# RMSNorm with every row written twice: the first load issued by itself, gamma in small pieces, and the first tile's rows dealt in another order

## The chip, the cores and the metric

The kernel runs on one core of a Trainium2 chip. The core has a vector engine (DVE), a scalar engine (ACT), a general engine (POOL), a matrix engine (PE, unused here) and a sync engine (SP) that only issues transfers and waits. All transfers, whichever engine issues them, are carried out by the same 16 DMA engines. The metric is the time of one execution on the device in microseconds (us). Before the change three runs took 239.03, 238.68 and 238.97 us: a median of 238.97.

## The reference

```python
x_rep = np.repeat(x, 2, axis=1)                      # x: (8, 512, 2048) float32
rms = np.sqrt((x_rep ** 2).mean(axis=-1, keepdims=True) + 1e-6)
return (x_rep / rms * gamma[None, None, :]).astype(np.float32)
```

There are 4096 rows of 2048 numbers. Each row is divided by its root mean square and multiplied by gamma, and the result is written twice, to two neighbouring rows of an output of 8192 rows. A row has 8 KB, so 33.6 MB are read and 67.1 MB are written.

## The kernel before

The rows are cut into four tiles of 1024 rows (`n` = 0 to 3). Each of the 128 partitions takes eight neighbouring rows of a tile: 64 KB that lie in one piece in memory. So a load is one transfer of 128 runs of 64 KB, 8.4 MB. The sixteen rows that a partition writes for a tile go out in two halves (`h` = 0, 1) of eight rows each, so a store is again 128 runs of 64 KB.

One buffer `y` of 24 rows a partition holds everything (line 46), in three places of eight rows, `first` (rows 0 to 7), `second` (8 to 15) and `third` (16 to 23). The order of instructions is written out by hand. `four(n, ...)` handles two tiles, and it is called twice, for tiles 0 and 1 and for tiles 2 and 3. In it:

- `load(n, first + K)` brings tile n into rows 4 to 11 (line 50), `constants()` runs the first time only, and `load(n + 1, third)` brings the next tile into rows 16 to 23. Both loads are issued by SP, one after the other, and share one queue with the stores.
- `squares` sums the squares of each row on ACT (line 63) and takes the root (line 67). `scale` takes the reciprocal on DVE (line 73) and multiplies row, reciprocal and gamma (line 75) into every second row of the output. `repeat` copies these rows to their neighbours, on ACT or DVE (line 82).
- `store` sends eight rows from SP (line 53). There are eight stores, two for each tile.

So the SP queue carries, in this order: load 0, load 1, four stores, load 2, load 3, four stores. SP issues in order: what waits there holds up all that stands behind it. Each of these twelve transfers is shared out to the 16 DMA engines, eight runs of 64 KB to each, which makes 96 runs an engine in all. A run appears in the profile as one packet.

`constants()` (lines 116 to 126) issues gamma from ACT in two pieces of 4 KB into partition 0 of `gamma_b` (line 118), which POOL then broadcasts to all partitions (line 122). DVE sets `eps_t` (line 123). ACT takes one square root of it into a tile of its own, `root`, whose value nobody uses (line 126): it makes ACT load its function table early.

Of the kernel before, what the change touches and what calls it, by code (L numbers as in the profile page):

```python
# [1 line left out]

# [4 lines left out]


@with_exitstack
def kernel(  # L10
    ctx: ExitStack,
    tc: tile.TileContext,
    x: bass.AP,
    gamma: bass.AP,
    out: bass.AP,
):
    nc = tc.nc
    P = nc.NUM_PARTITIONS
    f32 = mybir.dt.float32
    Act = mybir.ActivationFunctionType  # L20
    Alu = mybir.AluOpType

    B, S, D = x.shape
    Bo, So, Do = out.shape
    R = So // S
    assert R == 2 and D == Do and B == Bo and So == S * R
    eps = 1e-6
    inv_d = 1.0 / float(D)


    K = 4
    N = B * S
    ntiles = N // (P * K)
    assert N % (P * K) == 0 and ntiles == 8
    H = 2
    x_t = x.rearrange("b s d -> (b s) d").rearrange("(n p k) d -> n p k d", p=P, k=H * K)
    out_t = out.rearrange("b s d -> (b s) d").rearrange("(n p h j) d -> n h p (j d)", p=P, h=H, j=K * R)

    singles = ctx.enter_context(tc.tile_pool(name="singles", bufs=1))
    rows = ctx.enter_context(tc.tile_pool(name="rows", bufs=1))  # L40
    junk = ctx.enter_context(tc.tile_pool(name="junk", bufs=1, space=bass.MemoryType.PSUM))
    small = ctx.enter_context(tc.tile_pool(name="small", bufs=4))

    y = rows.tile([P, 3 * K * R, D], f32, name="y")
    first, second, third = 0, K * R, 2 * K * R

    def load(n, at):
        nc.sync.dma_start(out=y[:, at : at + H * K, :], in_=x_t[n])  # L50

    def store(n, h, to):
        nc.sync.dma_start(
            out=out_t[n, h], in_=y[:, to : to + K * R, :].rearrange("p j d -> p (j d)")
        )

    def squares(at, rows):

        n = len(rows)
        ss = small.tile([P, n], f32, name=f"ss{n}")  # L60
        for c, k in enumerate(rows):
            sq = junk.tile([P, D], f32, name="sq")
            nc.scalar.activation(  # L63
                out=sq[:], in_=y[:, at + k, :], func=Act.Square, accum_out=ss[:, c : c + 1]
            )
        rms = small.tile([P, n], f32, name=f"rms{n}")
        nc.scalar.activation(out=rms[:], in_=ss[:], func=Act.Sqrt, scale=inv_d, bias=eps_t[:])  # L67
        return rms

    def scale(at, to, rows, rms):  # L70
        n = len(rows)
        rstd = small.tile([P, n], f32, name=f"rstd{n}")
        nc.vector.reciprocal(out=rstd[:], in_=rms[:])  # L73
        for c, k in enumerate(rows):
            nc.vector.scalar_tensor_tensor(  # L75
                out=y[:, to + R * k, :], in0=y[:, at + k, :], scalar=rstd[:, c : c + 1],
                in1=gamma_b[:], op0=Alu.mult, op1=Alu.mult,
            )

    def repeat(to, k0, k1, copy):  # L80
        y_r = y[:, to + R * k0 : to + R * k1, :].rearrange("p (k r) d -> p k r d", r=R)
        copy(out=y_r[:, :, 1, :], in_=y_r[:, :, 0, :])  # L82

    ctx.enter_context(tc.manual_schedule())

    half = K // 2
    up, down = list(range(K)), list(range(K - 1, -1, -1))

    def four(n, constants):


        load(n, first + K)
        constants()
        load(n + 1, third)
        for rows in (up[:half], up[half:]):
            scale(first + K, first, rows, squares(first + K, rows))
        repeat(first, 0, half, nc.scalar.copy)
        repeat(first, half, K, nc.vector.tensor_copy)
        store(n, 0, first)
        scale(second, second, down, squares(second, down))  # L100
        repeat(second, half, K, nc.scalar.copy)
        repeat(second, 0, half, nc.vector.tensor_copy)
        store(n, 1, second)
        roots = [squares(third + h * K, up) for h in range(H)]
        scale(third, first, up, roots[0])
        repeat(first, 0, half, nc.scalar.copy)
        repeat(first, half, K, nc.scalar.copy)
        store(n + 1, 0, first)
        scale(third + K, third, up, roots[1])
        repeat(third, 0, K, nc.scalar.copy)  # L110
        store(n + 1, 1, third)

    gamma_b = singles.tile([P, D], f32, name="gamma_b")
    eps_t = singles.tile([P, 1], f32, name="eps_t")

    def constants():
        for c0 in (0, D // 2):
            nc.scalar.dma_start(
                out=gamma_b[0:1, c0 : c0 + D // 2],
                in_=gamma[c0 : c0 + D // 2].partition_broadcast(1),  # L120
            )
        nc.gpsimd.partition_broadcast(out_ap=gamma_b[:], in_ap=gamma_b[0:1, :])  # L122
        nc.vector.memset(eps_t, eps)  # L123

        root = singles.tile([P, 1], f32, name="root")
        nc.scalar.activation(out=root[:], in_=eps_t[:], func=Act.Sqrt)  # L126

    four(0, constants)
    four(2, lambda: None)


# [1 line left out]
_INS = ['x', 'gamma']  # L133
_OUTS = [((8, 1024, 2048), 'float32')]


# [23 lines left out]
```

## Time and profile before

| What | Value |
|---|---|
| median of three runs | 238.97 us (238.68 to 239.03) |
| span of the profiled execution | 236.7 us |
| time of the profiled execution itself | only the span is recorded; the median lies 2.2 us above it |
| DVE busy | 84.4 us, 36% of the span |
| ACT busy | 110.2 us, 47% |
| POOL busy | 2.5 us, 1% |
| SP's queue (q1): share of 16 DMA engines | 98.5%, 1728 packets, 100.66 MB |
| ACT's queue (q10), the two pieces of gamma | 4 packets, 0.01 MB |
| mean rate over the span | 425 GB/s |

A transfer leaves two kinds of packets: the data, 64 KB each here, and one of 4 bytes for each DMA engine when its share is done. In the lines on DMA the window asked for is cut into 40 equal slices, and a packet is put down, with all its bytes and all its time, to the slice in which it starts. In short slices, therefore, the row "GB/s" tells when packets begin: a packet of 65536 bytes in a slice of 0.04 us shows as 1638. For the same reason the shares of a short window can be over 100%. Share times length of the window times 16, over the number of packets, is the mean time of a packet.

### The profile page before, as it was taken

How to read it: one execution, taken by the hardware profiler on the slowest of the kernel's cores; microseconds unless marked ns; L12 is line 12 of the kernel's file. 1: busy time of each engine (PE TensorE's matmuls, PEld its weight loads, DVE VectorE, ACT ScalarE, POOL GpSimd, SP SyncE). 2: the span in 40 equal slices, each digit the busy share in tenths (PEclk: the TensorE clock that was granted, in tenths of full speed). 3: DMA queues.
4: the chain of work that ended last, by engine and by line, in shares of the span. 5: the costliest groups of instructions: out<-in, count | busy, mean ns of one | idle time of the engine just before them, and what ended most of it. 6: DMA issues, size and time to landing. Idle time of an engine off the chain costs nothing.

```text
span 236.7 us, 218 instructions
## 1 busy us (share of the span) xinstructions
DVE 84.4 (36%) x47; ACT 110.2 (47%) x86; POOL 2.5 (1%) x5
## 2 busy tenths in 40 slices
DVE  0000495594699400000000008929909992000000
ACT  2001989479998460000000058991999947300000
POOL 0210000000000000000000000000000000000000
DMA  9898989999898989899898989899898989899894
GB/s 355 355 532 354 532 354 487 399 443 443 365 520 354 532 354 509 377 465 421 354 532 354 532 354 520 367 399 487 354 532 354 520 365 509 376 465 421 365 520 177
DMA packets 1733, 100.68 MB, mean 425 GB/s; under 512 B 194, under 2 KB 194, under 8 KB 196
## 3 DMA queue, kind: packets, MB, share of 16 engines
q1 hardware_dynamic: 1728, 100.66, 98.5%
q10 hardware_dynamic: 4, 0.01, 0.0%
q14 instruction: 1, 0.01, 0.0%
HBM read 33.56 MB, written 67.11 MB: 425 GB/s over the span
## 4 chain that ended last, share of the span: by engine, by line
DMA 45%; ACT 26%; DVE 13%; issue 1%; DVEq 0%; SPq 0%
DMA y<-in_x_dram 26%; DMA out_dram<-y 20%; ACT sq L63 15%; DVE y L75 13%; ACT y L82 11%; ACT rms L67 1%; DVE rstd L73 0%; DVEq L75 0%; SPq L50 0%
## 5 line engine op out<-in xcount | busy, mean ns | idle before, releaser
L63 ACT ACTIVATE sq<-y 128x2048 f32<-128x2048 f32 x32 | 60.1, 1878 | 72.0 <-DMA y<-in_x_dram 71.3
L75 DVE SCALAR_TENSOR_TENSOR y<-y,rstd,gamma_b 128x2048 f32<-128x2048 f32 x32 | 73.8, 2349 | 2.1 <-DMA out_dram<-y 1.5
L82 ACT COPY y<-y 128x4096 f32<-128x4096 f32 (+1 forms) x10 | 42.6, 4283 | 19.5 <-DVE y L75 19.5
L73 DVE RECIPROCAL rstd<-rms 128x4 f32<-128x4 f32 (+1 forms) x10 | 1.7, 170 | 109.0 <-ACT rms L67 109.0
L82 DVE COPY y<-y 128x4096 f32<-128x4096 f32 x4 | 9.2, 2293 | 0.1
L63 ACT ACTIVATION_READ_ACCUMULATOR sq<-y 128x1 f32 x32 | 6.0, 186 | 0.0
L67 ACT ACTIVATE rms<-ss,eps_t 128x4 f32<-128x4 f32 (+1 forms) x10 | 3.0, 297 | 0.3
L122 POOL PARTITION_BROADCAST gamma_b<-gamma_b x1 | 2.3, 2294 | 10.2 <-DMA gamma_b<-in_gamma_dram 10.2
L126 ACT ACT_TABLE_LOAD x1 | 1.3, 1283 | 1.5 <-PEq L144 1.5
L123 DVE MEMSET eps_t<- 128x1 f32 x1 | 0.1, 59 | 0.8 <-PEq L144 0.8
L126 ACT ACTIVATE root<-eps_t 128x1 f32<-128x1 f32 x1 | 0.2, 203 | 0.0
L144 POOL MEMSET const-bfloat16-1.0<- 128x1 bf16 x1 | 0.1, 103 | 0.0
L144 POOL MEMSET const-float32-0.0<- 128x1 f32 x1 | 0.1, 100 | 0.2 <-issue 0.2
L144 POOL MEMSET const-uint8-127<- 128x1 uint8 x1 | 0.1, 102 | 0.0
L144 POOL MEMSET const-float32-1.0<- 128x1 f32 x1 | 0.1, 99 | 0.0
## 6 DMA issues: line engine op xcount, KB each, us to landing
out_dram<-y SPq DMA_DIRECT2D x8, 24.8
y<-in_x_dram SPq DMA_DIRECT2D x4, 39.2
gamma_b<-in_gamma_dram ACTq DMA_DIRECT2D x2, 4.0 KB
```

What stands on the lines that cost most here:

```text
L63: nc.scalar.activation(out=sq[:], in_=y[:, at + k, :], func=Act.Square, accum_out=ss[:, c : c + 1])
L67: nc.scalar.activation(out=rms[:], in_=ss[:], func=Act.Sqrt, scale=inv_d, bias=eps_t[:])
L73: nc.vector.reciprocal(out=rstd[:], in_=rms[:])
L75: nc.vector.scalar_tensor_tensor(out=y[:, to + R * k, :], in0=y[:, at + k, :], scalar=rstd[:, c : c + 1], in1=gamma_b[:], op0=Alu.mult, op ...
L82: copy(out=y_r[:, :, 1, :], in_=y_r[:, :, 0, :])
L122: nc.gpsimd.partition_broadcast(out_ap=gamma_b[:], in_ap=gamma_b[0:1, :])
L123: nc.vector.memset(eps_t, eps)
L126: nc.scalar.activation(out=root[:], in_=eps_t[:], func=Act.Sqrt)
L144: nc = _bacc.Bacc("TRN2", target_bir_lowering=False, num_devices=1)
```

## The change

Four things are edited.

- The first tile (`woven = (0,)`) is read and written through `x_w` and `out_w`. Partition p = 8w + q, with w from 0 to 15 and q from 0 to 7, now takes run 16q + w of the tile, where it took run p. The partitions with equal q in the 16 groups of eight thus take 16 neighbouring runs of 64 KB; before, eight neighbouring runs lay within one group, and the groups were 512 KB apart. On the memory's side the pattern has the dimensions 16 x 8 x 16384 elements; on the side of `y` it stays 128 partitions by 16384. The two stores of tile 0 write through the same order, with runs of 64 KB that are 128 KB apart from group to group (1 MB before). Tiles 1 to 3 keep their order.
- The unused square root writes `y[:, third, 0:1]`, the place that load 1 fills. Load 1 therefore waits on SP until ACT has done that square root.
- On ACT the table load and the square root now stand ahead of the DMA issues for gamma.
- Gamma comes as 16 pieces of 125 numbers (500 bytes) in one transfer and three transfers of 16 numbers (64 bytes) each. They land in rows 0 to 2 of partition 0 of `y`, with 1 KB between the starts of the 16 pieces, and two broadcasts on POOL, of 2000 and of 48 columns, bring them into `gamma_b`.

```diff
+    woven = (0,)
+    W = 16
+    x_w = x.rearrange("b s d -> (b s) d").rearrange("(n q w k) d -> n w q (k d)", w=W, q=P // W, k=H * K)
+    out_w = out.rearrange("b s d -> (b s) d").rearrange("(n q w h j) d -> n h w q (j d)", w=W, q=P // W, h=H, j=K * R)
+
     def load(n, at):
-        nc.sync.dma_start(out=y[:, at : at + H * K, :], in_=x_t[n])
+        to = y[:, at : at + H * K, :].rearrange("p k d -> p (k d)")
+        nc.sync.dma_start(out=to, in_=x_w[n] if n in woven else x_t[n].rearrange("p k d -> p (k d)"))
 
     def store(n, h, to):
         nc.sync.dma_start(
-            out=out_t[n, h], in_=y[:, to : to + K * R, :].rearrange("p j d -> p (j d)")
+            out=(out_w if n in woven else out_t)[n, h], in_=y[:, to : to + K * R, :].rearrange("p j d -> p (j d)")
         )
...
     gamma_b = singles.tile([P, D], f32, name="gamma_b")
+    G, E = 16, 3
+    C = D // G - E
+    gamma_s = y[0:1, 0:2, :].rearrange("p k (c d) -> p (k c) d", c=G // 2)
+    gamma_t = y[0:1, 2, :]
     eps_t = singles.tile([P, 1], f32, name="eps_t")
 
     def constants():
-        for c0 in (0, D // 2):
-            nc.scalar.dma_start(
-                out=gamma_b[0:1, c0 : c0 + D // 2],
-                in_=gamma[c0 : c0 + D // 2].partition_broadcast(1),
-            )
-        nc.gpsimd.partition_broadcast(out_ap=gamma_b[:], in_ap=gamma_b[0:1, :])
         nc.vector.memset(eps_t, eps)
 
-        root = singles.tile([P, 1], f32, name="root")
-        nc.scalar.activation(out=root[:], in_=eps_t[:], func=Act.Sqrt)
+        root = y[:, third, 0:1]
+        nc.scalar.activation(out=root, in_=eps_t[:], func=Act.Sqrt)
+        nc.scalar.dma_start(
+            out=gamma_s[0:1, :, :C],
+            in_=gamma[: G * C].rearrange("(p c d) -> p c d", p=1, c=G),
+        )
+        for c in range(E):
+            at = G * C + c * G
+            nc.scalar.dma_start(
+                out=gamma_t[0:1, c * G : (c + 1) * G],
+                in_=gamma[at : at + G].partition_broadcast(1),
+            )
+        nc.gpsimd.partition_broadcast(
+            out_ap=gamma_b[:, : G * C].rearrange("p (c d) -> p c d", c=G),
+            in_ap=gamma_s[0:1, :, :C],
+        )
+        nc.gpsimd.partition_broadcast(out_ap=gamma_b[:, G * C :], in_ap=gamma_t[0:1, : E * G])
```

More of the change, by code (lines that the diff above doesn't have):

```diff
@@ L113 @@
     gamma_b = singles.tile([P, D], f32, name="gamma_b")
+    G, E = 16, 3
+    C = D // G - E
+    gamma_s = y[0:1, 0:2, :].rearrange("p k (c d) -> p (k c) d", c=G // 2)
+    gamma_t = y[0:1, 2, :]
     eps_t = singles.tile([P, 1], f32, name="eps_t")
     def constants():
-        for c0 in (0, D // 2):
+        nc.vector.memset(eps_t, eps)
+        root = y[:, third, 0:1]
[6 more added lines that the diff above has]
+            at = G * C + c * G
             nc.scalar.dma_start(
-                out=gamma_b[0:1, c0 : c0 + D // 2],
-                in_=gamma[c0 : c0 + D // 2].partition_broadcast(1),
-            )
-        nc.gpsimd.partition_broadcast(out_ap=gamma_b[:], in_ap=gamma_b[0:1, :])
-        nc.vector.memset(eps_t, eps)
-        root = singles.tile([P, 1], f32, name="root")
-        nc.scalar.activation(out=root[:], in_=eps_t[:], func=Act.Sqrt)
+                out=gamma_t[0:1, c * G : (c + 1) * G],
+                in_=gamma[at : at + G].partition_broadcast(1),
+            )
+        nc.gpsimd.partition_broadcast(
[3 more added lines that the diff above has]
+        nc.gpsimd.partition_broadcast(out_ap=gamma_b[:, G * C :], in_ap=gamma_t[0:1, : E * G])
     four(0, constants)
```

## The prediction

> **What bounds the kernel now.** I read the page first: span, busy shares, queues.
>
> ```profile
> span 236.7 us, 218 instructions
> ...
> DMA  9898989999898989899898989899898989899894
> ...
> q1 hardware_dynamic: 1728, 100.66, 98.5%
> q10 hardware_dynamic: 4, 0.01, 0.0%
> ```
>
> SP's queue keeps the 16 DMA engines busy 98.5% of the span; no other engine passes 47%. So the time is the queue's length: when it starts, how long its packets take, when it ends. Next, the DMA view of a stretch in the middle, 24 to 60 us, which holds the end of load 1 and the start of the stores:
>
> ```profile
> DMA packets 255, 15.66 MB, mean 435 GB/s; under 512 B 16, under 2 KB 16, under 8 KB 16
> ...
> q1 hardware_dynamic: 255, 15.66, 100.4%
> ```
>
> There is no hole: 435 GB/s over 16 engines is 2.41 us for 64 KB. Then the start, in two windows that hold just the first and the second packet of each engine (1.6 to 3.2 us in slices of 0.04 us, where one packet shows as 1638; and 4.4 to 5.6 us in slices of 0.03 us, one packet 2185):
>
> ```profile
> GB/s 102 0 0 6554 3277 1638 1638 6554 1638 0 0 0 0 0 1638 0 0 0 0 0 0 0 0 1638 0 0 0 0 0 0 0 0 1638 0 0 0 0 0 0 0
> ...
> q1 hardware_dynamic: 16, 1.05, 187.7%
> q10 hardware_dynamic: 2, 0.00, 0.6%
> ```
>
> ```profile
> GB/s 0 0 0 0 0 0 0 0 0 4369 0 2185 0 2185 2185 2185 2185 2185 2185 2185 0 0 4369 2185 0 2185 0 0 2185 0 2185 0 0 0 0 0 0 0 0 0
> ...
> q1 hardware_dynamic: 16, 1.05, 201.6%
> ```
>
> Thirteen engines start between 1.72 and 1.96 us (mean of the slices 1.83); three are late, at 2.18, 2.54 and 2.90. The mean first packet takes 1.877 x 1.6 = 3.00 us, the mean second 2.016 x 1.2 = 2.42 us. The second packets start at 4.67 to 5.33, mean 4.96. Had all started like the thirteen and taken 2.42 us, the second would start at 4.16 to 4.36, mean 4.25. So the start loses 0.53 us on the first engine, 0.71 on the mean and 0.96 on the last, and nothing gives that back in a queue without holes.
>
> Are there other such places? At the turn from stores to load 2 (115.6 to 119.6 us, two packets an engine) and at the end (231.8 to 236.7, slices of 0.12 us, one packet 535):
>
> ```profile
> GB/s 0 655 1311 1966 2621 0 1311 1311 1311 0 0 0 0 0 0 0 0 0 0 0 0 0 0 0 0 0 0 0 1311 655 1966 1966 3932 655 0 0 0 0 0 0
> ...
> q1 hardware_dynamic: 48, 2.10, 128.3%
> ```
>
> ```profile
> GB/s 0 0 535 3210 2675 1070 535 0 0 0 535 0 0 0 0 0 0 0 0 0 0 0 0 0 0 0 0 0 0 0 0 0 0 0 0 0 0 0 0 0
> ```
>
> There 32 data packets take 1.283 x 4 x 16 / 32 = 2.57 us in the mean, 0.15 too much, twice: 0.3 us an engine. The change does not touch this place. At the end one engine starts its last packet at 233.0 to 233.2, some 0.4 us after the rest, and ends at 235.5; 1.2 us later the span is over. The floor is 1.74 + 96 x 2.42 = 234.1, so the slowest engine has lost 1.4 us altogether, of which the start is the largest part. Last, the timeline of the first microseconds and the chain, for the cover of what is moved:
>
> ```profile
> 0.72 0.76 ACTq L118 DMA_DIRECT2D gamma_b<-in_gamma_dram  x2
> 0.72 0.86 SPq L50 DMA_DIRECT2D y<-in_x_dram  x2
> ...
> 1.51 1.28 ACT L126 ACT_TABLE_LOAD   x1 [1.51 <-PEq L144]
> 2.80 0.20 ACT L126 ACTIVATE root<-eps_t 128x1 f32<-128x1 f32 x1
> 10.59 2.29 POOL L122 PARTITION_BROADCAST gamma_b<-gamma_b  x1 [10.16 <-DMA gamma_b<-in_gamma_dram]
> 22.61 1.88 ACT L63 ACTIVATE sq<-y 128x2048 f32<-128x2048 f32 x1 [19.61 <-DMA y<-in_x_dram]
> ...
> 27.27 4.62 DVE L75 SCALAR_TENSOR_TENSOR y<-y,rstd,gamma_b 128x2048 f32<-128x2048 f32 x2
> ...
> 39.15 0.35 SPq L53 DMA_DIRECT2D out_dram<-y  x1
> ```
>
> **The change part by part.**
>
> *Load 1 waits for the square root.* SP issued it about 0.43 us after load 0 (0.86 us for two). Now it waits for table load and root: 1.28 + 0.20 us, so done at 2.2 us if the table load moves up to 0.72, at 3.0 if it stays. Issue (0.43) and the way to the first packet (0.72 to 1.74: 1.0 us) bring it to the engines by 4.5 at the latest. They need it after eight packets, at 1.74 + 8 x 2.42 = 21.1. Cover 16.6 us; cost nothing. Behind it on SP stands the first store, at 39.15. ACT's four DMA issues for gamma (0.38 each, 1.5 us in all) end before 5 us; ACT sits idle until 22.61.
>
> *Gamma's bytes.* The two pieces before went to one engine: two packets, 4 KB and its completion, took 0.006 x 1.6 x 16 = 0.15 us, so 0.31 us for both pieces. Now every engine presumably carries 500 bytes and a completion, and one engine three times 64 bytes on top. Price: from 500/4096 of 0.15, which is 0.02, to 0.15 us an engine, and up to 0.45 more on the one with the three. I take 0.04 on each, nearest to the bytes. It is a loss: the engine that carried 0.31 before was one of sixteen, and the end shows no spread that only it would explain.
>
> *Gamma's arrival.* In the 6 to 12 us window the second piece's 4 KB start at 7.5 to 7.7, and POOL starts at 10.59: between data and completion lay one 64 KB packet. Four transfers are eight such turns. The first can fall at 6.6 (after two 64 KB packets), the eighth at 6.6 + 7 x 2.42 = 23.5; 0.5 us later POOL does the 48 columns, in 2.29 us at most (that is 2048 columns), so gamma is complete by 26.3 and probably by 24.5. The first broadcast, 2000 columns, runs at about 9.5 to 12. DVE needs gamma at 27.27 minus whatever load 0 gains, 26.3 to 26.7. It fits, though the cover shrinks from 14 us to two at best and none at worst; a miss of 1 us would still be taken by the next cover: store 0 is issued at 39.15 and needs 1.0 us to its first packet, and the earliest engine is free at 4.67 + 15 x 2.42 = 40.97, so 0.8 us to spare. After a full cure load 0 lands 0.96 earlier on the last engine and the earliest engine is free 0.53 earlier, which leaves 1.2 us.
>
> *The dealt order, load 0.* Nothing in the number or size of packets changes: eight of 64 KB an engine. What can change is the first round (3.00 against 2.42 us) and the three late starts. Bounds: a gain of 0.96 us (last engine, all cured) and none. That later packets of the same load, 0.65 us apart from first to last engine, run at 2.42 us says that the loss comes from sixteen engines reading in step, and that points to where they read; the late starts could be the other two transfers issued in the same microsecond. Both are edited. I take the mean engine, 0.71. Does the loss come back at load 1, not dealt, if the engines stay in step? Load 2 from its second packet on has most engines within 0.3 us (the slices 118.4 to 119.0 above) and its next packets (120.8 to 122 us: 16 packets, 201.5%) take 2.015 x 1.2 = 2.42 us; I take no return.
>
> *The dealt order, the stores of tile 0.* 16 packets an engine at a pitch of 128 KB instead of 1 MB. No row shows this pattern. Nearest rows: the stores in 24 to 60 us at 2.41 us; worst: 3.00 us, the first round. Ends: 0 and 16 x 0.58 = 9 us; I take 0, as all stores keep the same rate behind each other.
>
> Sum against this execution: 235.5 - 0.71 + 0.04 + 1.2 = 236.0 span, 0.67 less. The median of the runs is 2.2 us above this span; I leave those 2.2 as they are, within the runs' -0.3 and +0.1, and get 238.97 - 0.67 = **238.3 us**.
>
> [...]
>
> **The rivals.**
>
> *No cure* (238.6 to 239.4, likeliest 238.9). Sixteen engines that begin from rest, or that turn from writes to reads, lose time wherever they read. For it: load 2's turn is slow too though its engines are spread; the loss of round one may simply move to load 1. Against: load 1's round in the middle of a running queue shows none. Then at most the late starts are won, (0.35 + 0.71 + 1.07) / 16 = 0.13 us on the mean engine, and gamma's 0.04 is lost.
>
> *The dealt pattern is slower, packet by packet* (the other side). 24 packets an engine, load 0 and two stores, go through the 16 x 8 pattern. It costs 24 us for each us a packet gains in length; from (0.67 + 0.48) / 24 = 0.05 us, 2% of a packet, it turns the forecast into a loss beyond what can be measured. With the worst mean of the trace, 3.00 us, it is 24 x 0.58 = 14 us, 253 us. For it: no row has this pattern. Against: in the middle, loads with 512 KB and stores with 1 MB from group to group run alike at 2.41 us.
>
> *Gamma too late.* If each small packet waits for two 64 KB packets instead of one, the eighth comes at 6.6 + 7 x 4.84 = 40.5, the first multiplication slips by some 15 us and the queue stands dry for about 14: 253 us. Against: the one packet between 7.5 and 10.59.
>
> **How the numbers follow.** Two runs of this kernel can differ by 0.35 us; 0.2% (0.48 us, so 238.49 and 239.45) is about what tells a change from none. Forecast 0.50, own range 237.9 to 238.7; of it 0.39 lies below 238.49 and 0.11 within. No cure 0.30: 0.07 faster, 0.16 same, 0.07 slower. Slower pattern 0.14, gamma late 0.03, another small loss (the one engine with the extra pieces, an unlucky last engine) 0.03: all slower. Sum: faster 0.46, same 0.27, slower 0.27. The range 237.9 to 240.0 holds the first two cases and the small losses, 0.82; the 14 us cases stay outside.
>
> **What would show it.** In the first-round window sixteen starts within 0.3 us and a share that gives 2.4 to 2.5 us a packet; second starts at 4.15 to 4.45; the last packet starting 0.7 us earlier than 233.1. Gamma right: POOL's second broadcast done before 26 us. Wrong: a first round still at 3 us; packets above 2.42 us in load 1 around 21 us; q1's share in 2 to 20 us or 40 to 80 us with fewer packets than 16 a 2.42 us; POOL ending after 26.5 and store 0 issued later than 39.15.

## The result and the profile after

The changed kernel takes 301.64 us (median of four runs, 300.92 to 304.0) against 238.9 us: a ratio of 1.265, interval 1.263 to 1.268, so 62.7 us more. The prediction was 238.3 us with a range to 240.0. It missed both the size and the sign.

The profiled execution is the one of 300.92 us, with a span of 298.8, so 2.1 us lie outside the span. Its page:

```profile
span 298.8 us, 223 instructions
...
GB/s 246 176 193 228 149 272 421 421 351 211 175 246 219 254 219 185 263 193 290 421 447 439 421 412 386 430 439 421 421 421 439 421 421 430 430 421 421 421 421 281
DMA packets 1767, 100.68 MB, mean 337 GB/s; under 512 B 230, under 2 KB 230, under 8 KB 230
...
q1 hardware_dynamic: 1728, 100.66, 98.0%
```

SP's queue has the same 1728 packets and the same bytes, and the DMA engines are still busy 98.0% of the span. No hole has opened: the packets themselves have become longer. The row "GB/s" shows where. It starts at about 200, goes up to 421 for a while, falls back to about 220 and from the middle on stays near 420. The table by stage, cut near the end of load 0, of load 1 and of the two stores of tile 0 (the columns are busy time and number of instructions of DVE, ACT and POOL, the clock of the matrix engine, the share of the 16 DMA engines, and GB/s), first after, then before:

```profile
0.00:42.00 42.00, 0.06 (x1) 1.49 (x2) 2.43 (x5) 1.00 0.96 200
42.00:60.00 18.00, 11.43 (x7) 15.14 (x14) 0.32 (x1) 1.00 0.97 411
60.00:140.00 80.00, 30.76 (x17) 39.40 (x29) 0.00 (x0) 1.00 1.01 233
140.00:298.80 158.80, 42.18 (x23) 54.33 (x42) 0.00 (x0) 1.00 0.97 417
```

```profile
0.00:22.00 22.00, 0.06 (x1) 1.49 (x2) 2.48 (x5) 1.00 0.98 414
22.00:41.00 19.00, 11.85 (x7) 17.51 (x16) 0.00 (x0) 1.00 0.94 407
41.00:80.00 39.00, 30.33 (x16) 29.86 (x27) 0.00 (x0) 1.00 1.03 445
80.00:236.70 156.70, 42.19 (x23) 61.30 (x43) 0.00 (x0) 1.00 0.98 424
```

Load 0 takes 20 us longer and runs at half the rate; load 1, in its plain order, is as fast as before; the two stores of tile 0 take 41 us longer, again at half the rate; the rest differs by 2 us. The slow stages are exactly the three transfers that go through the 16 x 8 pattern. The window 11.2 to 13.2 us holds the third packet of load 0 on each of the 16 DMA engines:

```profile
q1 hardware_dynamic: 16, 1.05, 255.6%
```

The mean packet takes 2.556 x 2 = 5.11 us, 2.11 times the 2.42 us of before. The first round, where a gain was forecast (1.6 to 3.2 us, slices of 0.04 us, one packet 1638):

```profile
GB/s 0 0 0 0 0 0 0 0 0 0 0 0 0 0 4915 6554 1638 0 0 0 0 0 0 0 0 0 0 0 0 0 1638 6554 1638 3277 0 0 0 0 0 0
...
q1 hardware_dynamic: 16, 1.05, 292.4%
```

Eight engines start at 2.16 to 2.28 us and eight at 2.80 to 2.96, where thirteen had started before 1.96; the mean first packet takes 2.924 x 1.6 = 4.68 us, where 2.42 was forecast and 3.00 measured before. Gamma is a passenger: 16 of its small packets start in the window 5.5 to 8.5 us, among the second 64 KB packets, and 16 of 4 bytes in the window 11.2 to 13.2 us, among the third, one packet of 5.11 us later:

```profile
13.72 2.24 POOL L141 PARTITION_BROADCAST gamma_b<-y  x1 [13.30 <-DMA y<-in_gamma_dram]
43.33 0.32 POOL L145 PARTITION_BROADCAST gamma_b<-y  x1 [27.36 <-DMA y<-in_gamma_dram]
...
60.49 17.23 SPq L59 DMA_DIRECT2D out_dram<-y  x2
```

The second broadcast ran at 43.33 (23.06 in the undealt change below), just ahead of the first work on load 0 (ACT's first square starts at 43.97).

### The profile page after: what moved, and what is told of

Same layout as the page of the kernel before. It is cut to its first block, busy times and chain, and to the rows that moved or that the text cites. A ratio compares the mean times of both kernels' runs of the same rounds, so it can differ in the third digit from the quotient of the medians.

```text
span 298.8 us, 223 instructions
## 1 busy us (share of the span) xinstructions
DVE 84.4 (28%) x47; ACT 110.4 (37%) x86; POOL 2.8 (1%) x6
## 3 DMA queue, kind: packets, MB, share of 16 engines
q1 hardware_dynamic: 1728, 100.66, 98.0%
## 4 chain that ended last, share of the span: by engine, by line
DMA 65%; DVE 12%; ACT 11%; issue 1%; DVEq 0%
DMA out_dram<-y 37%; DMA y<-in_x_dram 28%; DVE y L81 12%; ACT y L88 6%; ACT sq L69 5%; ACT rms L73 0%; DVE rstd L79 0%; DVEq L81 0%
## 5 line engine op out<-in xcount | busy, mean ns | idle before, releaser
L69 ACT ACTIVATE sq<-y 128x2048 f32<-128x2048 f32 x32 | 60.1, 1878 | 115.6 <-DMA y<-in_x_dram 114.9
L81 DVE SCALAR_TENSOR_TENSOR y<-y,rstd,gamma_b 128x2048 f32<-128x2048 f32 x32 | 73.8, 2348 | 21.5 <-DMA out_dram<-y 20.9
L141 POOL PARTITION_BROADCAST gamma_b<-y x1 | 2.2, 2244 | 13.3 <-DMA y<-in_gamma_dram 13.3
L145 POOL PARTITION_BROADCAST gamma_b<-y x1 | 0.3, 323 | 27.4 <-DMA y<-in_gamma_dram 27.4
```

Of the source, the lines that this page charges most:

```text
L69: nc.scalar.activation(out=sq[:], in_=y[:, at + k, :], func=Act.Square, accum_out=ss[:, c : c + 1])
L81: nc.vector.scalar_tensor_tensor(out=y[:, to + R * k, :], in0=y[:, at + k, :], scalar=rstd[:, c : c + 1], in1=gamma_b[:], op0=Alu.mult, op ...
L141: nc.gpsimd.partition_broadcast(out_ap=gamma_b[:, : G * C].rearrange("p (c d) -> p c d", c=G), in_ap=gamma_s[0:1, :, :C],)
L145: nc.gpsimd.partition_broadcast(out_ap=gamma_b[:, G * C :], in_ap=gamma_t[0:1, : E * G])
```

## The experiments

Two theories of the loss stood at first. A: the 16 x 8 pattern hands each DMA engine a whole group of eight neighbouring partitions, and engines in step then meet at the same ways into the buffer. B: sixteen neighbouring runs of 64 KB, read or written at the same time, collide in memory. C, a third, put part of it on gamma and the held load. No row of the profile shows any of them. Where no ratio is given, the time is that of one run, with the runs of before at 238.7 us beside it.

### Which part of the change it is

Everything but the deal:

```diff
-    woven = (0,)
+    woven = ()
```

> The change without its dealt order: load 1 held behind the square root, gamma in small pieces, all tiles in their plain order. Both theories of the loss, A (the 16 x 8 pattern makes the DMA engines take whole groups of eight partitions, and engines in step get in each other's way at the buffer) and B (16 neighbouring 64 KB runs at the same time collide in memory), lay the loss on the dealt order and expect the time of before, 238.9 us, within 0.5 us. Theory C (the loss, or a good part, comes from gamma's late third and fourth small transfer, 43.3 us in the profile after, and the held load) expects 5 us or more above before. From the prediction's first step (late starts come from the transfers issued in the same microsecond): the three late first packets disappear, and the time falls by 0.1 to 0.5 us.

Measured: 238.41 us against 238.69, ratio 0.9982, interval 0.9971 to 0.9993. C falls: without the deal nothing is lost. But one step of the prediction is not confirmed: the first round stays bad.

```profile
GB/s 0 0 0 4915 3277 3277 4915 0 3277 1638 1638 0 1638 0 0 0 0 0 0 0 0 0 0 0 0 0 0 1638 0 0 0 0 0 0 0 0 0 0 0 0
...
q1 hardware_dynamic: 16, 1.05, 197.0%
```

Two of the three late starts are gone; one engine is still late, at 2.70 us. The mean first packet takes 1.970 x 1.6 = 3.15 us, no better than 3.00 before.

The deal alone, in the kernel before, with `constants()` untouched (the edits of the next two experiments together):

> The kernel before with the dealt order of tile 0 alone, load and both stores; gamma and load 1 as before. A and B expect the whole loss: 24 packets an engine at 5.1 instead of 2.42 us, 64 us, so 299 to 304 us. C expects less than 297 us.

Measured: 302.48 us, ratio 1.266 (1.263 to 1.270). The deal is the whole loss.

The deal in the load alone:

```diff
...
-        nc.sync.dma_start(out=y[:, at : at + H * K, :], in_=x_t[n])
+        to = y[:, at : at + H * K, :].rearrange("p k d -> p (k d)")
+        nc.sync.dma_start(out=to, in_=x_w[n] if n in woven else x_t[n].rearrange("p k d -> p (k d)"))
```

> The kernel before with load 0 alone dealt; the stores of tile 0 are plain, so its output rows come out in another order. If load and stores lose alike, packet by packet, load 0 costs 8 x 2.69 = 21.5 us: 260 us, with load 0's packets at 5.1 us and all others at 2.42. If the stores carry more than their share (their packets in the profile after are mixed with those of load 1), less than 257.

Measured: 260.89 us, 22.2 more.

And in the two stores alone:

```diff
...
-            out=out_t[n, h], in_=y[:, to : to + K * R, :].rearrange("p j d -> p (j d)")
+            out=(out_w if n in woven else out_t)[n, h], in_=y[:, to : to + K * R, :].rearrange("p j d -> p (j d)")
```

> The kernel before with the 16 x 8 pattern in the two stores of tile 0 alone (output rows in another order than the reference's). The deal of both took 63.8 us more, the load alone 22.2. If the two add up, the stores cost 41.6: 280 us. At 16 packets of 5.1 instead of 2.42 us it would be 43: 281.7.

Measured: 280.63 us, 41.9 more. 22.2 + 41.9 = 64.1 against 63.8 for both together: the costs add up, about 2.7 us for each of the 8 + 16 packets of an engine (2.8 in the load, 2.6 in the stores).

### Addresses or pattern

The same 16 x 8 pattern with the groups 1 MB apart, so that no neighbouring runs are read at once:

```diff
+    far = x.rearrange("b s d -> (b s) d")[0:2048, :].rearrange("(w r k) d -> w r (k d)", w=16, k=H * K)[:, 0:8, :]
...
-        nc.sync.dma_start(out=y[:, at : at + H * K, :], in_=x_t[n])
+        to = y[:, at : at + H * K, :].rearrange("p k d -> p (k d)")
+        nc.sync.dma_start(out=to, in_=far if n == 0 else x_t[n].rearrange("p k d -> p (k d)"))
```

> Load 0 through a 16 x 8 pattern whose groups of eight lie 1 MB apart in memory and whose runs within a group are neighbours, as in the plain order (it reads other rows of x, so tile 0's output is not the reference's). Theory A expects the same loss as with the dealt load, packets of 5.1 us and about 260 us: the pattern is the same, only the addresses differ. Theory B expects packets near 2.42 us and about 239 us, since no neighbouring runs are read at the same time.

Measured: 261.84 us. The window 11.2 to 13.6 us, with 16 data packets:

```profile
q1 hardware_dynamic: 16, 1.05, 213.8%
```

That is 2.138 x 2.4 = 5.13 us a packet. B falls for the load; the stores were not tested in this way. The counter-test reads close together through the plain pattern:

```diff
+    near = bass.AP(x.tensor, 0, [[2 * D, P], [1, H * K * D]])
...
-        nc.sync.dma_start(out=y[:, at : at + H * K, :], in_=x_t[n])
+        to = y[:, at : at + H * K, :].rearrange("p k d -> p (k d)")
+        nc.sync.dma_start(out=to, in_=near if n == 0 else x_t[n].rearrange("p k d -> p (k d)"))
```

> Load 0 plain over 128 partitions, but the 64 KB runs of neighbouring partitions start only 16 KB apart and overlap, so all engines read within 2 MB at the start (tile 0's input and output are not the reference's). Theory A expects all packets after the first at 2.42 us and 238 to 239.5 us. Theory B expects packets well above 2.42 us in load 0 and 245 us or more. For the first round (3.00 us before): if it is slow because of where the engines read, it changes here, to under 2.7 us or above 3.3; if it is slow because sixteen engines begin at once, it stays at 2.9 to 3.1.

Measured: 240.19 us, ratio 1.005 (1.003 to 1.007): packets of 2.42 us after the first round, so no collision of the size in question. It is still 1.5 us slower than before, a little more than theory A had allowed. And the first round is slower, not cured: 204.5% of 1.6 us, 3.27 us a packet. By the bound written down (under 2.7 or above 3.3) this settles nothing on its own; it leaves no support for the idea that neighbouring addresses help at the start.

### Which partitions are written at once

No deal at all; load 0 is only cut by partitions:

```diff
-        nc.sync.dma_start(out=y[:, at : at + H * K, :], in_=x_t[n])
+        c = 64 if n == 0 else P
+        for p0 in range(0, P, c):
+            nc.sync.dma_start(out=y[p0 : p0 + c, at : at + H * K, :], in_=x_t[n, p0 : p0 + c])
```

> No dealt order: load 0 as two plain transfers, partitions 0 to 63 and then 64 to 127, so that all 16 DMA engines write into one half of the buffer at a time. Same runs, same addresses as before in each half. Theory A (engines that write into too few places of the buffer at once) expects load 0's packets near 5 us, as in the profile after, and 256 to 262 us. Theory B (neighbouring addresses) expects 2.42 us and about 239 us, as runs are as far apart as before or half as far. [...]

Measured: 260.68 us, and in the window 11.2 to 13.6 us

```profile
q1 hardware_dynamic: 16, 1.05, 214.0%
```

2.140 x 2.4 = 5.14 us: the length of the dealt packets, in a load whose rows, runs and addresses are all as before. With `c = 32`:

> Load 0 as four plain transfers of 32 partitions. If what counts is how many partitions are written at once, packets take twice as long as with halves, near 10 us, and the run 290 to 300 us. If 32 neighbouring partitions reach as many ways into the buffer as 64 do, packets take as long as with halves, near 5 us, and the run 256 to 262 us. [...]

Measured: 260.08 us, and 2.143 x 2.4 = 5.14 us a packet in the window 10.8 to 13.2 us; 32 partitions are no slower than 64. With `c = 16`:

> Load 0 as eight plain transfers of 16 partitions. Halves and quarters both took 5.1 us a packet. [...] If the loss comes from a transfer of fewer than 128 partitions as such, packets stay at 5.1 us and the time near 260.

Measured: 294.93 us, far from 260: packets have not stayed at 5.1 us. In the window 18 to 23 us 16 data packets (and 16 of 4 bytes) took

```profile
q1 hardware_dynamic: 32, 1.05, 187.2%
```

1.872 x 5 = 9.36 us each, 6.94 more than 2.42. Eight such packets are 8 x 6.94 = 55.5 us, which leads to 294. So 16 partitions move 16 x 65536 / 9.36 = 112 GB/s, 32 and 64 partitions move 204, and 128 move 433. The sharpest test takes 64 partitions from the middle first, 32 to 95, then the outer ones:

```diff
-        nc.sync.dma_start(out=y[:, at : at + H * K, :], in_=x_t[n])
+        for p0, p1 in ((32, 96), (0, 32), (96, P)) if n == 0 else ((0, P),):
+            nc.sync.dma_start(out=y[p0:p1, at : at + H * K, :], in_=x_t[n, p0:p1])
```

> Load 0 as three plain transfers: partitions 32 to 95 first, then 0 to 31 and 96 to 127. If 64 partitions are slow as such (halves: 5.1 us), all of load 0 is slow and the time is near 260 us. [...]

Measured: 251.01 us. The window 7 to 8.6 us holds the third packet of each engine, from the middle 64 partitions, and the window 16 to 19 us the sixth, from the outer ones:

```profile
q1 hardware_dynamic: 16, 1.05, 151.2%
```

```profile
q1 hardware_dynamic: 16, 1.05, 170.8%
```

1.512 x 1.6 = 2.42 us and 1.708 x 3 = 5.12 us. Sixty-four partitions can run at full rate or at half; it depends on which.

### Which outer counts are slow

If unequal outer counts were enough, any such pattern would be slow. With 64 x 2 for the load:

```diff
+    x_v = x.rearrange("b s d -> (b s) d").rearrange("(n q v k) d -> n v q (k d)", v=64, q=2, k=H * K)
...
-        nc.sync.dma_start(out=y[:, at : at + H * K, :], in_=x_t[n])
+        to = y[:, at : at + H * K, :].rearrange("p k d -> p (k d)")
+        nc.sync.dma_start(out=to, in_=x_v[n] if n == 0 else x_t[n].rearrange("p k d -> p (k d)"))
```

> Load 0 dealt by another unequal pattern: partition 2v + q takes run 64q + v, so the memory side is 64 x 2 x 16384 against 128 x 16384 at the buffer (tile 0's rows are read in another order than its stores write them). Theory A in its wider form (whenever the outer counts of the two sides differ, each DMA engine is given a block of eight neighbouring partitions) expects 5.1 us a packet in load 0 and 259 to 262 us. If only the 16 x 8 pattern, one run of eight for each of 16 engines, does it, packets stay at 2.42 us and the time at 238.5 to 239.5.

Measured: 238.81 us; the window 7 to 8.5 us, 16 data packets:

```profile
q1 hardware_dynamic: 16, 1.05, 161.3%
```

1.613 x 1.5 = 2.42 us. The wider form of theory A falls. Three dimensions with 128 on the outside on both sides:

```diff
+    x_v = x.rearrange("b s d -> (b s) d").rearrange("(n g p k) d -> n p g (k d)", g=2, p=P, k=K)
...
-        nc.sync.dma_start(out=y[:, at : at + H * K, :], in_=x_t[n])
+        to = y[:, at : at + H * K, :].rearrange("p (g k) d -> p g (k d)", g=2)
+        nc.sync.dma_start(out=to, in_=x_v[n] if n == 0 else x_t[n].rearrange("p (g k) d -> p g (k d)", g=2))
```

> Load 0 with a third dimension too, but 128 on the outside on both sides: each partition's eight rows come as two runs of 32 KB that lie 4 MB apart in memory (again tile 0 in another order of rows). If any pattern of three dimensions is slow, load 0's packets take 2.5 us for 32 KB and the time is near 260 us. Theory A expects 1.21 us for 32 KB and 238.5 to 239.5 us.

Measured: 238.77 us, and packets of 32 KB take 1.014 x 1.2 = 1.22 us after the first (4.4 to 5.6 us, 16 packets). Three dimensions are not the trouble either. Last the whole change with 32 x 4, in which a block that stays together is four partitions wide:

```diff
-    W = 16
+    W = 32
```

> The whole change with W = 32 in place of 16: partition 4v + q takes run 32q + v, load and stores, so the pattern in memory is 32 x 4 and neighbouring blocks of four partitions take neighbouring runs. Theory A, narrowed (an engine is given blocks of four partitions as long as the outer count has 32 parts to deal; with 16 parts it gets eight neighbouring partitions in one), expects 2.42 us a packet throughout and the time of the undealt change, 238.1 to 238.8 us. If every outer count under 64 groups the engines by eight, 299 to 304 us as measured for 16. If neighbouring addresses cured the first round after all, under 238.0.

Measured: 240.77 us, ratio 1.0087 (1.0073 to 1.0101). The window 7 to 9 us, 16 data packets:

```profile
q1 hardware_dynamic: 16, 1.05, 120.9%
```

1.209 x 2 = 2.42 us: the long packets are gone, and 61 of the 62.7 us with them. So an outer count of 32 (and of 64, tried in the load alone) keeps the packets at 2.42 us, and 16 does not. That would fit theory A as it was narrowed: blocks of four partitions to an engine where the pattern can be dealt that finely, and eight neighbours where it has only 16 parts. But which engine carries which partition is in no record of these traces, so this link is the author's reading, not shown; nor does a run show why eight neighbours to an engine should halve the rate. And the runs that cut by partitions are all loads; that the stores lose in the same way is argued from their like cost a packet.

One packet stands out in the dealt load: packet 5 of an engine, the first of the second four. In load 0 of the changed kernel (21.8 to 23.2 us) it takes 3.524 x 1.4 = 4.93 us, where the others after the first take 5.11:

```profile
q1 hardware_dynamic: 16, 1.05, 352.4%
```

The plain loads that are cut by partitions have such a shorter packet too. These windows of 2 us each hold 16 data packets and 16 of 4 bytes: packet 5 with halves (21.5 to 23.5 us), packet 5 and packet 7 with quarters (21 to 23 and 31 to 33), packet 7 with the middle first (21.5 to 23.5):

```profile
q1 hardware_dynamic: 32, 1.05, 246.7%
```

```profile
q1 hardware_dynamic: 32, 1.05, 246.6%
```

```profile
q1 hardware_dynamic: 32, 1.05, 257.2%
```

```profile
q1 hardware_dynamic: 32, 1.05, 246.4%
```

That is 4.93, 4.93, 5.14 and 4.93 us. The packet is short where the engines move from one half of the buffer to the other: to partition 64 with halves and quarters, from 0 to 31 on to 96 to 127 with the middle first. It is not short where they stay in one half, as at packet 7 with quarters (from 64 to 95 on to 96 to 127). With eighths the rounds after the first start five slices of 1.85 us apart in the window 2 to 76 us, about 9.3 us; a packet shorter by 0.2 us would not show there. With the deal, too, something changes between the fourth and the fifth packet; what it is, no run shows.

But the 32 x 4 kernel is no gain either: 2.4 us slower than the same change without a deal. Its first round:

```profile
GB/s 0 0 0 0 0 0 0 0 0 0 0 0 0 0 6554 1638 4915 3277 1638 3277 1638 0 0 0 0 1638 0 0 0 0 0 0 1638 0 0 0 0 0 0 0
...
q1 hardware_dynamic: 16, 1.05, 205.4%
```

The first packets start at 2.16 us, 0.44 after those of the plain pattern, and take 2.054 x 1.6 = 3.29 us, 0.14 more than undealt. The turn to load 2 (115.6 to 122 us) is slower as well: 32 data packets at 0.881 x 6.4 x 16 / 32 = 2.82 us, 0.8 us an engine above 2.42 in two packets, against 48 at 1.182 x 6.4 x 16 / 48 = 2.52 undealt, 0.3 us an engine in three. Over all its packets an engine is busy 0.982 x 238.8 = 234.5 us, 1.4 more than 0.985 x 236.7 = 233.1 in the kernel before, and it starts 0.44 us later; where the rest goes was not traced.

### The small gain

The hold alone, gamma in its two pieces of 4 KB:

```diff
     def constants():
+        nc.vector.memset(eps_t, eps)
+        root = y[:, third, 0:1]
+        nc.scalar.activation(out=root, in_=eps_t[:], func=Act.Sqrt)
         for c0 in (0, D // 2):
...
-        nc.vector.memset(eps_t, eps)
-
-        root = singles.tile([P, 1], f32, name="root")
-        nc.scalar.activation(out=root[:], in_=eps_t[:], func=Act.Sqrt)
```

> The kernel before with load 1 held behind the square root and the table load ahead of gamma's issue; gamma in two pieces of 4 KB as before, no dealt order. If the three late first packets (2.18, 2.54, 2.90 us) come from the second load or gamma being issued in the same microsecond, all sixteen start within 0.3 us, and the time falls by 0.1 to 0.5 us. If not, the late starts stay and the time is that of before within 0.2 us.

Measured: 238.74 against 238.68 us, ratio 1.0003 (0.9994 to 1.0011). Three first packets are still late (2.15, 2.29 and 2.62 us), so they do not come from the second load being issued beside the first. Gamma is excluded only in part. None of its packets runs in the window of 1.6 to 3.2 us, but its issue hardly moved: although it stands behind the table load and the square root, ACT issued it while the table load ran, at 0.88 us against 0.72 before (0.90 in the changed kernel).

```profile
0.88 0.74 ACTq L121 DMA_DIRECT2D gamma_b<-in_gamma_dram  x2
```

The small pieces alone:

```diff
-        root = y[:, third, 0:1]
+        root = singles.tile([P, 1], f32, name="root")[:]
```

(with `woven = ()` as well)

> Gamma in small pieces, and ACT's order, as in the change; load 1 not held, no dealt order. With the undealt change 0.2 to 0.4 us under before and the hold alone at nothing: if the small pieces carry that gain, 238.2 to 238.5 us; if it takes both, or was chance, 238.6 to 238.9.

Measured: 238.31 against 238.66 us, ratio 0.9988 (0.9979 to 0.9997). And the undealt change again:

> The undealt change once more, beside the same runs of before: 0.1 to 0.6 us faster if the first result (ratio 0.9982) holds; no difference beyond 0.1 us if it was chance.

Measured: 238.4 against 238.72 us, ratio 0.9986 (0.9977 to 0.9995). In three comparisons of three the kernel with small pieces is 0.3 us faster, though each interval ends just below 1. The hold adds nothing that can be seen, and ACT's new order is in the hold's run too, where it gives nothing. Why the small pieces give 0.3 us stays open: the profiled spans, 236.6, 236.3 and 237.0 us, scatter more than the gain.

These two, the undealt change and the small pieces alone, are the fastest versions measured, 0.3 us under the kernel before.

## Why the prediction was wrong

- **The stores of tile 0 (the step that failed, first part).** The prediction put the pattern between 0 and 9 us and took 0, "as all stores keep the same rate behind each other". Measured: 41.9 us. The stores of tile 0 stand behind each other too, and their stage moved 233 GB/s against 445 before: the rate kept before was that of the plain pattern, and standing in a queue does not keep it.
- **The dealt order, load 0 (second part).** "Nothing in the number or size of packets changes" was right, and the conclusion that only the first round can change was not. It took a gain of 0.71 us, with "none" as its worst end; measured was a loss of 22.2. The stores' worst end, 9 us, came from the slowest round of the trace, 3.00 us a packet. The rows of before all come from transfers with 128 partitions outermost on both sides, and none of them could bound a pattern of another kind. What the runs showed in its place: through the 16 x 8 pattern a packet of load 0 takes 5.11 us instead of 2.42, about as long as in a plain load into half of the partitions at a time (5.14).
- **The rival on the other side** named the place of the loss, 24 packets an engine that each take longer, and had it right, at a chance of 0.14. Its price, 24 x 0.58 = 14 us, was too small because of the same bound: a packet grew by 2.69 us, and 24 x 2.69 = 64.6, against 62.7 measured. What makes a packet longer was not shown: that the 16 x 8 pattern gives the engines whole groups of partitions, where the plain one did not, is the author's reading.
- **The start.** The 0.71 us lost in the first round was read rightly, but nothing in the change wins it back. Holding load 1 leaves late starts, reading nearby leaves 3.27 us a packet, the undealt change 3.15. For "that points to where they read" no run gives support; the rival "no cure" was right on this. What makes the first round slow was not found.
- **Load 1's wait** was free, as costed: 1.0003.
- **Gamma's arrival** was right where the packets are 2.42 us: in the undealt change POOL starts the second broadcast at 23.06 us, against 23.5 plus 0.5, and the first at 10.73, against about 9.5.

```profile
10.73 2.25 POOL L141 PARTITION_BROADCAST gamma_b<-y  x1 [10.30 <-DMA y<-in_gamma_dram]
23.06 0.32 POOL L145 PARTITION_BROADCAST gamma_b<-y  x1 [10.08 <-DMA y<-in_gamma_dram]
```

- **Gamma's bytes** were costed as a loss of 0.04 us; the small pieces win 0.3.
- **The range.** It left the case of 14 us and more outside, at 0.14 of the chance, and that case came. (The cases that it holds add up to 0.83; the prediction has 0.82.)

## What to carry to other kernels

When an access pattern of a transfer is rearranged, look at the outermost count on both sides and ask which partitions the DMA engines will touch at the same moment (a load that wrote partitions 0 to 63 first took 5.14 us a packet, the load over all 128 took 2.42); a trace of the old pattern says nothing about it, since neither bytes nor packets change. Keep the 128 partitions outermost on both sides, or try the pattern on one transfer first: 64 x 2 and 32 x 4 kept 2.42 us a packet here, though 32 x 4 still made the kernel 2.4 us slower, and 16 x 8 took 5.11. And where no row of the trace shows the new pattern, its worst row is no end for the range: 3.00 us a packet was taken, 5.11 came.

## What was not expected of the hardware

- Sixty-four partitions are fast or slow by their place: 32 to 95 at 2.42 us a packet, 0 to 63 at 5.14. Thirty-two run as fast as 64 of one half, 5.14 us a packet with quarters.
- In slices of 0.04 us, the first packets started between 2.12 and 2.20 us wherever load 0 was dealt by 16 x 8, 64 x 2 or 32 x 4, against 1.68 to 1.76 with the plain 128 partitions. The deal is not needed for it: two plain loads cut by partitions also began late, halves at 2.04 to 2.08 and the middle first after 2.00, while quarters and eighths began at 1.72 to 1.76. The reason stays open.
- The loss of the first round looks more like a fixed time than a share of a packet: 32 KB packets took 1.087 x 1.6 = 1.74 us instead of 1.22 in the first round (0.52 more, in one run), 64 KB packets 3.00 instead of 2.42 (0.58 more; 0.73 in the undealt change).
